# HGRN2 intra-chunk attention in a decoder trunk: the third level's strips run with the fourth level's from kept copies, and the first two levels run in the tick of the first inverse products

## The chip, the cores and the metric

One core of one Trainium2 chip. The metric is the device time of one execution of the whole program, in microseconds (us). All tensors are float32. The large products are done on TensorE in a split form (each operand as a high and a low part, three products per pair), so TensorE's stream of 128x128 by 128x512 matmuls is most of the program.

## What is computed

A decoder layer over 2048 tokens of width 1024 (one layer, batch 1): one input projection feeds four heads of gated DeltaNet and four heads of HGRN2, whose outputs go through one output projection; then an MLP with squared ReLU and a gated embedding. The change lies in the HGRN2 heads. Cut to what matters:

```python
def hgrn2_chunked(q, k, v, log_f):          # here: chunks of 16; the kernel uses chunks of 128
    bc = cumsum(log_f, within the chunk)
    def step(s, (q_n, k_n, v_n, b_n)):
        pair = exp(where(causal, b_n[:, i] - b_n[:, j], -inf))
        att = einsum('bihd,bjhd,bijhd->bhij', q_n, k_n, pair)
        o = att @ v_n + (q_n * exp(b_n)) @ s
        s = s * exp(b_last) + (k_n * exp(b_last - b_n))^T @ v_n
        return s, o
```

The decay between token i and token j has its own value in each of the 128 dimensions, so att is no plain product. The kernel builds it by levels. At level s = 1, 2, 4, ..., 64 a token block of 2s is cut in an early and a late half; queries of the late half meet keys of the early half, each first multiplied by its own decay up to the boundary between the halves. A mask then picks the entries of att that belong to that level.

## The kernel before

**Stages.** An embedding projection, the mixer (the first 1035 us or so), the output projection, the MLP and the gates. The mixer goes through 4 token quarters q of 512 tokens and 4 head pairs h. Each pair (one DeltaNet head and one HGRN2 head, written here as head q_h, so 1_3 is quarter 1, pair 3) has 8 projection works of 24 large matmuls (L1174), in the order k, q, z, v of the DeltaNet head, then f, i, q, g of the HGRN2 head.

**Ticks.** Each work is cut into 3 ticks of 8 large matmuls; a tick thus holds one third of a work, and a pair 24 ticks. Between the large matmuls, `half()` and `tick()` call generators that stand on an agenda: the two head mixers `gdn_mixer` and `hgrn_mixer` of the pair whose projections are running or have just run. The step n of `hgrn_mixer` runs in tick `B_STEPS[n]` and the step n of `gdn_mixer` in tick `A_STEPS[n]`, counted from the tick in which the pair's projections began (the last pair has its own tables `A_LAST`, `B_LAST`, and the first pair has `A_FIRST` for its DeltaNet head). TensorE's order is thus written by hand. SyncE's (SP's) queue, which issues the DMAs, is written by hand in the mixer too. The orders of VectorE (DVE) and ScalarE (ACT) are set when the program is built, by the tile scheduler; they are fixed lists when the program runs.

**The steps of `hgrn_mixer` around the change.** 
- Tick 24 copies the late queries of level 0 to `both[:, 0]` (tile `hb`), and does the first products on DVE. Tick 26 copies the late queries of level 1 to `both[:, 1]`.
- Tick 28 is a bunch of strips for levels 0 and 1. A strip is a small matmul (`strip`, L631) that uses 32 of TensorE's 128 columns: four of them with different column positions fill four row groups of a PSUM tile. Level 0's diagonal goes to `of_h` (4 strips), and its other part and level 1 go to `at_all` (16 strips; 4 and 16 calls give 8 and 32 matmul records in the profile, since a matmul on float32 data shows as two records). Then DVE takes `of_h` (L901) and `at_all` (L903, both with a mask), multiplies the keys by the decay (L926), copies level 1 into att under a mask (L931), multiplies the queries (L930), and forms the decays of the next level (L937). ACT copies the keys for the next level to a packed tile `keys` (L929; this tile has two buffers).
- Tick 30 (level 2, s = 4) and tick 32 (level 3, s = 8) each run 8 strips from `keys` and the queries, and then the same DVE and ACT operations for the next level. Levels 4 to 6 follow in ticks 34, 36 and 38.
- In the DeltaNet head, tick 30 holds the 8 strips `psp5` (a product for the inverse of a triangular matrix) and tick 32 holds the 12 strips `pst5` and `psx5` of the next step of that inverse. In the first pair `psp5` is in tick 32 and the other two in tick 34. In the last pair (`A_LAST`, `B_LAST`) levels 0 and 1 are in tick 26, level 2 in tick 27, level 3 and `psp5` in tick 28.

So in most pairs there are three bunches of strips in these ticks: levels 0 and 1 alone; `psp5` and level 2; `pst5`, `psx5` and level 3. `at_all` is one PSUM bank of 512 columns. A level uses half of it (`lev % 2`), so level 2 and level 3 use different halves.

**Others that run in the same ticks.** DVE and ACT also do the convolution of the DeltaNet projections (L565 on ACT, L569 on DVE, then L570 on DVE and L578 or L575/L576 on ACT), the splits into high and low parts (L176 on ACT, L177 on DVE: of the weights `w` in the first quarter, when they come from HBM, and of the squared head outputs `hl`), the norms (L286, L667, L669, L620) and, from quarter 1 on, `down_sums` (L1128 to L1135), which loads blocks of w_down by DMA and adds and subtracts them on DVE for the MLP. Its calls stand on the agenda at fixed ticks of their own.

Of the kernel before, what the change touches and what calls it, by code (L numbers as in the profile page):

```python
# [13 lines left out]
U32 = mybir.dt.uint32  # L14
AF = mybir.ActivationFunctionType
# [5 lines left out]
P = 128  # L21
# [3 lines left out]
QT = 512  # L25
# [31 lines left out]
           + tuple(o for c in range(38, 54, 4) for o in (c, c + 1.5, c + 2.5))  # L57
           + (53, 55, 57, 59, 60, 61, 65, 66))
I_STEPS = (22,)
B_STEPS = (24, 26, 28, 30, 32, 34, 36, 38, 40, 42, 44, 45, 46, 48, 50, 52, 53, 54, 58, 59)  # L60


A_AHEAD = (-12, -6)
# [33 lines left out]
def trunk(ctx, tc, x, xT, pT, vecs, w_in, w_ab, gdn_a_log, gdn_dt_bias, w_out, w_up, w_down,  # L97
# [363 lines left out]
    with mixers as mctx:  # L461
# [164 lines left out]
        def rows_of(g):  # L626
            return slice(g * SB, (g + 1) * SB)

        def strip(g, out, lhsT, rhs):

            PE.matmul(out, lhsT, rhs, start=True, stop=True, tile_position=(0, g * SB))  # L631
# [223 lines left out]
        def hgrn_mixer(q, h, live):  # L855
# [14 lines left out]
            def by_half(t, s):  # L870
                return t.rearrange("p (a n s) -> p a n s", a=2, s=s)
# [10 lines left out]
            for lev, s in enumerate(LEVELS):  # L882
# [4 lines left out]
                if lev == 1:  # L887
# [6 lines left out]
                    for c in range(NC):  # L894
                        for j in range(NB):
# [31 lines left out]
                if 2 * s < P:  # L927
                    keys = m2.tile([P, QT // 2], F32, tag="keys", name=f"keys_{n}_{lev}")
                    S.activation(keys.rearrange("p (n a s) -> p a n s", a=2, s=2 * s), side(k, QT, 2 * s, False), AF.Copy)  # L929
                V.tensor_tensor(side(qq, QT, s, True), side(qq, QT, s, True), early, ALU.mult)  # L930
                V.copy_predicated(side_of_chunks(columns_of, s, True),  # L931
                                  mask[lev].rearrange("p (a n s) -> p a n s", a=2, s=s).bitcast(U32)[:, :, None]
                                  .broadcast_to([P, 2, 2, P // (2 * s), s]),
                                  ps.rearrange("p a b (n s) -> p a b n s", s=s))
                gv = g.rearrange("p (n two) -> p n two", two=2)
                g2 = mt(f"gg_{n}_{lev}", f"gg{lev}", 1, (P, nb // 2))
                V.tensor_tensor(g2, gv[:, :, 0], gv[:, :, 1], ALU.mult)  # L937
# [1045 lines left out]
```

## Time and profile before

| what | value |
|---|---|
| median of 3 runs | 2637.18 us |
| lowest and highest run | 2633.91 and 2642.8 us |
| the profiled execution, its own time | 2643.16 us |
| its span in the trace | 2641.4 us |
| PE busy | 2601.6 us (98%) |
| DVE, ACT busy | 1964.7 us (74%), 1464.2 us (55%) |
| POOL busy | 137.2 us (5%) |
| granted TensorE clock | 1.000 |

Busy shares are means over the whole program. The change acts only in the mixer, so what matters there is the order on PE, and who is waited for at the strips. In rows of the timeline, the columns are the start in us, the time from the first start to the last end of the group in us, the engine, the line and operation, out<-in, the shape and the number of instructions; a bracket at the end is the idle time just before on that engine, and what ended it. Matmuls are pipelined, so the time of a stretch of n large matmuls contains one tail of about 0.4 us, and starts are compared with starts.

### The profile page before, as it was taken

What the parts mean: (1) busy time and instruction counts of PE and PEld (TensorE: products, weight loads), DVE (VectorE), ACT (ScalarE), POOL (GpSimd) and SP (SyncE); (2) the same over time, 40 slices, a digit from 0 to 9 for tenths busy, and PEclk for the clock granted to TensorE, in tenths of its full rate; (3) what the DMA queues carried; (4) which work ended last, traced back from release to release, by engine and by line L of the source; (5) the groups of instructions that cost most, each with busy time, mean ns of one, the idle gap of its engine ahead of it and who ended that gap; (6) DMA issues with size and microseconds to landing.
All of it is one profiled execution on the core that took longest, in us unless ns stands there. A gap on an engine that the chain in (4) does not pass through costs nothing.

```text
span 2641.4 us, 43911 instructions
## 1 busy us (share of the span) xinstructions
PE 2601.6 (98%) x15593; PEld 2143.3 (81%) x15593; DVE 1964.7 (74%) x4032; ACT 1464.2 (55%) x2991; POOL 137.2 (5%) x147
## 2 busy tenths in 40 slices
PE   8999999999999999999999999999999999999999
PEld 5788788878878888787888888888888888888887
DVE  7788777776777777578988778767877765477776
ACT  7675655465555555566566465555455465565322
POOL 0000000000000000110000000001000001101000
PEclk9999999999999999999999999999999999999999
DMA  8777777767767675774675576665644375677664
GB/s 278 276 266 259 253 264 247 239 215 253 242 201 250 228 233 165 222 211 142 216 230 185 183 231 221 214 211 187 220 151 168 138 245 188 200 253 251 204 218 134
DMA packets 267788, 573.87 MB, mean 217 GB/s; under 512 B 55578, under 2 KB 60152, under 8 KB 250416
## 3 DMA queue, kind: packets, MB, share of 16 engines
q1 hardware_dynamic: 265264, 566.86, 64.5%
q0 software_dynamic: 2304, 4.20, 0.9%
q8 instruction: 123, 2.02, 0.3%
q14 instruction: 97, 0.79, 0.1%
HBM read 410.57 MB, written 160.37 MB: 216 GB/s over the span
## 4 chain that ended last, share of the span: by engine, by line
PE 76%; DMA 10%; DVE 7%; ACT 3%; issue 3%; SPq 1%; POOL 0%; DVEq 0%; ACTq 0%; POOLq 0%
PE d L1208 23%; PE u L1208 23%; PE mm L1174 17%; PE mmg L1208 7%; DMA cache_in<-w 2%; DMA sys_g<-ud_g 1%; PE mme L203 1%; DMA ud_g<-u_g 1%; DMA raw_out<-in_w_out_dram 1%; DMA mixT<-mixd 1%; DMA xs<-in_x_dram 1%; DMA yod<-yo 1%; DVE w L177 1%; DVE pr_g L744 0%; DMA wd<-in_w_down_dram 0%
## 5 line engine op out<-in xcount | busy, mean ns | idle before, releaser
L1174 PE MATMUL mm<-xt,w 128*128 128x512 f32 x3072 | 785.6, 401 | 2.6 <-DVE acc_vg L569 1.3
L1174 PEld LDWEIGHTS mm<-xt,w 128*128 128x128 f32 x3072 | 552.6, 188 | 109.1 <-ACT w L176 1.7
L1208 PE MATMUL d<-db,da 128*128 128x512 f32 x2688 | 612.8, 389 | 0.0
L1208 PE MATMUL u<-t,wu 128*128 128x512 f32 x2604 | 591.2, 389 | 0.0
L1208 PEld LDWEIGHTS d<-db,da 128*128 128x128 f32 x2688 | 504.5, 188 | 104.8
L1208 PEld LDWEIGHTS u<-t,wu 128*128 128x128 f32 x2604 | 488.7, 188 | 101.5
L230 DVE TENSOR_TENSOR db<-db 128x512 fp32r<-128x512 f32 x224 | 159.5, 712 | 62.0 <-ACT db L229 60.9
L1606 DVE TENSOR_TENSOR u<-u,u 128x512 f32<-128x512 f32 x224 | 150.5, 683 | 52.7 <-PE u L1208 51.2
L229 ACT ACTIVATE db<-db 128x512 fp32r<-128x512 f32 x224 | 140.9, 629 | 69.1 <-DMA db<-hid 66.7
L1208 PE MATMUL mmg<-h2T,wg 128*128 128x512 f32 (+1 forms) x792 | 174.7, 383 | 0.0
L1208 PEld LDWEIGHTS mmg<-h2T,wg 128*128 128x128 f32 x792 | 145.5, 188 | 29.1
L1649 ACT ACTIVATE u<-u 128x512 f32<-128x512 f32 x128 | 80.8, 631 | 155.0 <-DVE u L1606 154.5
L177 DVE TENSOR_TENSOR da<-da 128x512 fp32r<-128x512 f32 x128 | 94.5, 738 | 91.8 <-ACT da L176 89.9
L176 ACT ACTIVATE da<-da 128x512 fp32r<-128x512 f32 x128 | 80.6, 630 | 129.0 <-DMA da<-sumd 110.9
L1208 PE MATMUL mmo<-mixT,w_out 128*128 128x512 f32 x600 | 138.9, 391 | 3.6 <-DVE w_out L177 1.6
L1208 PEld LDWEIGHTS mmo<-mixT,w_out 128*128 128x128 f32 x600 | 112.1, 188 | 29.4 <-DVE w_out L177 2.9
L176 ACT ACTIVATE wu<-a 128x512 fp32r<-128x512 f32 x124 | 75.1, 623 | 53.3 <-DMA a<-in_w_up_dram 51.5
L177 DVE TENSOR_TENSOR wu<-a,wu 128x512 fp32r<-128x512 f32 x124 | 86.0, 695 | 8.0 <-ACT wu L176 7.5
L177 DVE TENSOR_TENSOR da<-dr,da 128x512 fp32r<-128x512 f32 x96 | 68.3, 711 | 22.4 <-ACT da L176 21.0
L1650 ACT ACTIVATE u<-u 128x512 f32<-128x512 f32 x128 | 80.4, 628 | 3.0
L246 POOL TENSOR_TENSOR acc_y<-acc_y,sq_y 128x512 f32<-128x512 f32 x28 | 37.6, 1341 | 759.9 <-ACT sq_y L245 759.9
L176 ACT ACTIVATE da<-dr 128x512 fp32r<-128x512 f32 x96 | 60.5, 630 | 29.4 <-DMA dr<-in_w_down_dram 21.1
(401 smaller groups left out, 3677.2 us busy)
## 6 DMA issues: line engine op xcount, KB each, us to landing
w<-cache_in SPq DMA_DIRECT2D x96, 1024.0 KB
db<-hid SPq DMA_DIRECT2D x224, 256.0 KB
cache_in<-w SPq DMA_DIRECT2D x32, 1024.0 KB
hid<-u SPq DMA_DIRECT2D x128, 256.0 KB
da<-sumd SPq DMA_DIRECT2D x128, 256.0 KB
a<-in_w_up_dram SPq DMA_DIRECT2D x124, 256.0 KB
hid<-ht SPq DMA_DIRECT2D x96, 256.0 KB
dr<-in_w_down_dram SPq DMA_DIRECT2D x96, 256.0 KB
```

The source lines that it names most:

```text
L176: S.activation(t[:, 0], raw, AF.Copy)
L177: eng.tensor_tensor(t[:, 1], raw, t[:, 0], ALU.subtract)
L203: PE.matmul(ps, a, b, start=i == 0, stop=i == n - 1)
L229: S.activation(t[:, 0], plain(t), AF.Copy)
L230: V.tensor_tensor(t[:, 1], plain(t), t[:, 0], ALU.subtract)
L246: eng.tensor_tensor(acc, acc, sq, ALU.add)
L1174: PE.matmul(ps, *terms[i], start=i == 0, stop=i == nt - 1)
L1208: PE.matmul(ps, a, b, start=start, stop=stop)
L1606: V.tensor_tensor(c[new], c[old], ps, ALU.add)
L1649: S.activation(c[k], c[k], AF.Relu)
L1650: S.activation(c[k], c[k], AF.Square)
```

## The change

Three things in `hgrn_mixer` and its table.

1. `B_STEPS` begins with 24, 27, 30, 31, 32 where it began with 24, 26, 28, 30, 32. The copy of level 1's late queries goes from tick 26 to 27, the bunch of levels 0 and 1 from tick 28 to 30, and level 2's step from tick 30 to 31. The later ticks are as before. `B_LAST` is not changed.
2. Level 2's step issues no strips. Instead ACT copies the late queries of level 2 to `both[:, 0]`, which level 0 has used (new line L907; 256 columns, 16 such copies in the program), and the name `first_keys` holds on to level 2's keys. The DVE products and the ACT copy of the keys for level 3 follow as before.
3. Level 3's step first runs level 2's 8 strips, from the kept keys and the copied queries, into the half of `at_all` that level 2 always had, then its own 8 strips. DVE then copies both levels into att under their masks, one after the other.

```diff
-B_STEPS = (24, 26, 28, 30, 32, 34, 36, 38, 40, 42, 44, 45, 46, 48, 50, 52, 53, 54, 58, 59)
+B_STEPS = (24, 27, 30, 31, 32, 34, 36, 38, 40, 42, 44, 45, 46, 48, 50, 52, 53, 54, 58, 59)
...
+                elif lev == 2:
+                    S.activation(by_half(both[:, 0], s), side(qq, QT, s, True), AF.Copy)
+                    ps, first_keys = None, keys
                 else:
 
+                    if lev == 3:
+                        for c in range(2):
+                            for j in range(NB):
+                                at_j = both.offset + c * P // 2 + j * SB // 2
+                                strip(j, second[rows_of(j), :, c, near[j]], first_keys[:, c * P + j * SB : c * P + (j + 1) * SB],
+                                      bass.AP(both.tensor, at_j, [list(both.ap[0]), [P, 2], [1, SB // 2]]))
...
-                V.copy_predicated(side_of_chunks(columns_of, s, True),
-                                  mask[lev].rearrange("p (a n s) -> p a n s", a=2, s=s).bitcast(U32)[:, :, None]
-                                  .broadcast_to([P, 2, 2, P // (2 * s), s]),
-                                  ps.rearrange("p a b (n s) -> p a b n s", s=s))
+                if lev == 2:
+                    second = at_all[:, : QT // 2].rearrange("p (a b n) -> p a b n", a=2, b=2)
+                else:
+                    picked = [(lev, s, ps)]
+                    if lev == 3:
+                        picked.insert(0, (2, LEVELS[2], second))
+                    for l, s_l, ps_l in picked:
+                        V.copy_predicated(side_of_chunks(columns_of, s_l, True),
...
```

The number of strips, of masked copies and of products is as before. Behind the change the lines are shifted: the keys' product L926 is L935, the keys' copy L929 is L938, the queries' product L930 is L939, the masked copy L931 is L947, the large matmul L1174 is L1190, and L1131 to L1135 of `down_sums` are L1147 to L1151.

**PE, head 0_1.** Before, in the ticks 28 to 32 of the head (`mm_0` and `mm_12` are projection works of the next pair, whose large matmuls are the stream; `at_all_81` and `of_h_86` are the two PSUM tiles; the numbers behind a name count its tiles):

```order
L1174 MATMUL mm_0_0_2_1998<-xt0_5_547,w_0_0_2_1830 128x512
L631 MATMUL of_h_86<-att_h0_1_1935,one_102 32x4x16 x4
L631 MATMUL at_all_81<-hb_h0_1_1936,qk_h0_1_1659 32x2x16 x16
L1174 MATMUL mm_0_0_2_1998<-xt0_5_547,w_0_0_2_1830 128x512 x2
...
L1174 MATMUL mm_12_0_2_2093<-xt0_2_498,w_12_0_2_1907 128x512 x2
L631 MATMUL psp5_g0_1_2104<-xn_g0_1_1976,um5_584 32x32 x8
L631 MATMUL at_all_81<-qk_h0_1_1659,keys_h0_1_1_2046 32x2x16 x8
...
L631 MATMUL psx5_g0_1_2180<-part5_586,xt_g0_1_1975 32x32 x2
L631 MATMUL at_all_81<-qk_h0_1_1659,keys_h0_1_2_2126 32x2x16 x8
```

And now, over the same ticks:

```order
L1190 MATMUL mm_0_0_2_1998<-xt0_5_547,w_0_0_2_1831 128x512 x3
...
L1190 MATMUL mm_12_0_2_2065<-xt0_2_498,w_12_0_2_1908 128x512 x2
L631 MATMUL psp5_g0_1_2076<-xn_g0_1_1977,um5_584 32x32 x8
L631 MATMUL of_h_86<-att_h0_1_1936,one_102 32x4x16 x4
L631 MATMUL at_all_81<-hb_h0_1_1937,qk_h0_1_1660 32x2x16 x16
...
L631 MATMUL psx5_g0_1_2173<-part5_586,xt_g0_1_1976 32x32 x2
L631 MATMUL at_all_81<-hb_h0_1_1937,keys_h0_1_1_2112 32x2x16 x8
L631 MATMUL at_all_81<-qk_h0_1_1660,keys_h0_1_2_2138 32x2x16 x8
```

Three places where strips break into the large matmuls have become two; the first of these now holds `psp5` with levels 0 and 1, the second holds levels 2 and 3.

**ACT, head 0_1.** Before, from the first keys' copy of the head (for level 2) to the third (for level 4) and what follows; `w_16` is a weight that is split in these ticks, `osq` and `hl` are of a DeltaNet head of the pair before:

```order
L929 ACTIVATE keys_h0_1_1_2046<-qk_h0_1_1659 128x2x32x4
L611 ACTIVATE osq_g0_0_2069<-of_g_85 128x512
L929 ACTIVATE keys_h0_1_2_2126<-qk_h0_1_1659 128x2x16x8
...
L176 ACTIVATE hl_g0_0_2073<-osq_g0_0_2069 128x512
L785 ACTIVATE part5_586<-psp5_g0_1_2104 32x2x32 x4
L929 ACTIVATE keys_h0_1_3_2209<-qk_h0_1_1659 128x2x8x16
L176 ACTIVATE w_16_0_2_2086<-raw_16_0_2_1994 128x1024
L286 ACTIVATE osq_g0_0_2069<-nrm_g0_0_2144 1x512
L667 ACTIVATE jk_g0_2_0_2159,ssk_g0_2_2150<-t_kg0_2_2153 128x128
```

And now:

```order
L176 ACTIVATE hl_g0_0_2045<-osq_g0_0_2041 128x512
L785 ACTIVATE part5_586<-psp5_g0_1_2076 32x2x32 x4
L907 ACTIVATE hb_h0_1_1937<-qk_h0_1_1660 128x256
L176 ACTIVATE w_16_0_2_2058<-raw_16_0_2_1994 128x1024
L578 ACTIVATE y_qg0_2_2057<-acc_qg0_2_2050 128x512
L938 ACTIVATE keys_h0_1_1_2112<-qk_h0_1_1660 128x2x32x4
L286 ACTIVATE osq_g0_0_2041<-nrm_g0_0_2130 1x512
L667 ACTIVATE jk_g0_2_0_2152,ssk_g0_2_2143<-t_kg0_2_2146 128x128
...
L938 ACTIVATE keys_h0_1_2_2138<-qk_h0_1_1660 128x2x16x8
```

The keys' copies for levels 2 and 3 have moved from ahead of the split of `w_16` to behind it, with the convolution's L578, the norm's L286 and four L667 (three of them are left out above) between the new query copy and the second keys' copy.

**DVE, head 1_3.** Before, around the keys' product for level 3 (which is the second L926 of the head); `gcol`, `tail` are gate values of the next quarter, and the block sums of `down_sums` (L1131) come behind the last row shown here:

```order
L926 TENSOR_TENSOR qk_h1_3_6296<-qk_h1_3_6296,gg_h1_3_1_6697 128x2x32x4
L569 SCALAR_TENSOR_TENSOR acc_kg2_0_6730<-mm_4_2_0_6646,cols_96,acc_kg2_0_6730 128x511
L930 TENSOR_TENSOR qk_h1_3_6296<-qk_h1_3_6296,gg_h1_3_1_6697 128x2x32x4
L570 TENSOR_TENSOR acc_kg2_0_6730<-acc_kg2_0_6730,bound_582 128x3
L931 COPY_PREDICATED att_h1_3_6577<-cst_93,at_all_81 128x2x32x4
L549 COPY gcol_2_6800<-ps_gb_2_6795 128x144
L926 TENSOR_TENSOR qk_h1_3_6296<-qk_h1_3_6296,gg_h1_3_2_6777 128x2x16x8
```

And now:

```order
L569 SCALAR_TENSOR_TENSOR acc_kg2_0_6708<-mm_4_2_0_6652,cols_96,acc_kg2_0_6708 128x511
L903 TENSOR_TENSOR att_h1_3_6584<-at_all_81,cst_93 128x2x128
L570 TENSOR_TENSOR acc_kg2_0_6708<-acc_kg2_0_6708,bound_582 128x3
L935 TENSOR_TENSOR qk_h1_3_6303<-qk_h1_3_6303,gg_h1_3_0_6586 128x2x64x2
L947 COPY_PREDICATED att_h1_3_6584<-cst_93,at_all_81 128x2x64x2
L939 TENSOR_TENSOR qk_h1_3_6303<-qk_h1_3_6303,gg_h1_3_1_6769 128x2x32x4
L549 COPY gcol_2_6799<-ps_gb_2_6794 128x144
L1147 TENSOR_TENSOR wd6_1_6703<-wd6_1_6703,wd6_0_6702 128x512
L935 TENSOR_TENSOR qk_h1_3_6303<-qk_h1_3_6303,gg_h1_3_1_6769 128x2x32x4
```

The work of level 1 and the keys' product for level 3 have moved behind the third L569, and the first block sum of `down_sums` (L1147, which is L1131 before) now stands ahead of the keys' product for level 3.

More of the change, by code (lines that the diff above doesn't have):

```diff
@@ L930, in hgrn_mixer @@
                 V.tensor_tensor(side(qq, QT, s, True), side(qq, QT, s, True), early, ALU.mult)
-                V.copy_predicated(side_of_chunks(columns_of, s, True),
-                                  mask[lev].rearrange("p (a n s) -> p a n s", a=2, s=s).bitcast(U32)[:, :, None]
-                                  .broadcast_to([P, 2, 2, P // (2 * s), s]),
-                                  ps.rearrange("p a b (n s) -> p a b n s", s=s))
+                if lev == 2:
[6 more added lines that the diff above has]
+                        V.copy_predicated(side_of_chunks(columns_of, s_l, True),
+                                          mask[l].rearrange("p (a n s) -> p a n s", a=2, s=s_l).bitcast(U32)[:, :, None]
+                                          .broadcast_to([P, 2, 2, P // (2 * s_l), s_l]),
+                                          ps_l.rearrange("p a b (n s) -> p a b n s", s=s_l))
                 gv = g.rearrange("p (n two) -> p n two", two=2)
```

## The prediction

> **What bounds the kernel now.** I read the page first: the span, the engines' busy shares, the granted clock and the chain that ended last, then the group of the mixer's large matmuls.
>
> ```profile
> span 2641.4 us, 43911 instructions
> PE 2601.6 (98%) x15593; PEld 2143.3 (81%) x15593; DVE 1964.7 (74%) x4032; ACT 1464.2 (55%) x2991; POOL 137.2 (5%) x147
> PEclk9999999999999999999999999999999999999999
> PE 76%; DMA 10%; DVE 7%; ACT 3%; issue 3%; SPq 1%; POOL 0%; DVEq 0%; ACTq 0%; POOLq 0%
> L1174 PE MATMUL mm<-xt,w 128*128 128x512 f32 x3072 | 785.6, 401 | 2.6 <-DVE acc_vg L569 1.3
> ```
>
> PE is busy for 98% of the span at full granted clock, and its 3072 large matmuls of the mixer wait only 2.6 us in all. So a change here pays by what it takes out of PE's own stream, and costs by every wait it puts in: there are few waits now, and those of the strips are mostly hidden. The next view is PE's timeline through the three bunches of one ordinary head (1_1).
>
> ```profile
> 412.91 1.16 PE L1174 MATMUL mm<-xt,w 128*128 128x512 f32 x4
> 414.00 0.32 PE L631 MATMUL of_h<-att_h,one 128*32 128x64 f32 x8
> 414.14 0.48 PE L631 MATMUL at_all<-hb_h,qk_h 128*32 128x32 f32 x32
> 414.54 1.19 PE L1174 MATMUL mm<-xt,w 128*128 128x512 f32 x4
> ...
> 416.16 3.02 PE L1174 MATMUL mm<-xt,w 128*128 128x512 f32 x12
> 419.11 0.33 PE L631 MATMUL psp_g<-xn_g,um 128*32 128x32 f32 x16
> 419.25 0.31 PE L631 MATMUL at_all<-qk_h,keys_h 128*32 128x32 f32 x16
> 419.50 2.09 PE L1174 MATMUL mm<-xt,w 128*128 128x512 f32 x8
> ...
> 422.24 2.10 PE L1174 MATMUL mm<-xt,w 128*128 128x512 f32 x8
> 424.27 0.28 PE L631 MATMUL pst_g<-xt_g,part 128*32 128x32 f32 x9
> ...
> 424.78 1.43 PE L1174 MATMUL mm<-xt,w 128*128 128x512 f32 x5
> ```
>
> And the first head, whose level 2 stands alone, with a long stretch ahead of it:
>
> ```profile
> 97.76 7.89 PE L1174 MATMUL mm<-xt,w 128*128 128x512 f32 x34
> ...
> 106.12 3.92 PE L1174 MATMUL mm<-xt,w 128*128 128x512 f32 x16
> 109.97 0.33 PE L631 MATMUL at_all<-qk_h,keys_h 128*32 128x32 f32 x16
> 110.23 2.11 PE L1174 MATMUL mm<-xt,w 128*128 128x512 f32 x8
> ```
>
> One step of the stream is (7.89 - 0.40) / 33 = 0.227 us, with 0.40 for the last one (the group's mean of 401 ns). What a bunch costs is the time from the start of the stretch ahead to the start of the stretch behind, less 0.227 per large matmul. Levels 0 and 1 alone: 414.54 - 412.91 - 4 x 0.227 = 0.72. `psp5` with level 2: 419.50 - 416.16 - 12 x 0.227 = 0.62. `pst5`, `psx5` and level 3: 424.78 - 422.24 - 8 x 0.227 = 0.72. Level 2 alone: 110.23 - 106.12 - 16 x 0.227 = 0.48. Sixteen strip records take 0.14 (419.11 to 419.25), so 0.34 of that 0.48 is paid for breaking into the stream at all, however many strips follow.
>
> **The change part by part.** *PE.* No strip is added or removed; one break of three goes. After it, tick 30 should cost 0.62 - 0.14 + (0.72 - 0.34) = 0.86 and tick 32 0.72 + 0.14 = 0.86: together 1.72 where 2.06 stood, so **0.34 us less per head**. In the last head the lone level 2 bunch goes with a wait of its own:
>
> ```profile
> 1024.80 0.33 PE L631 MATMUL at_all<-qk_h,keys_h 128*32 128x32 f32 x16 [0.56 <-ACT keys_h L929]
> ```
>
> That is 0.34 + 0.56 = 0.90. Gross gain: 15 x 0.34 + 0.90 = **6.0 us**, if nothing new is late.
>
> *What gets tighter.* Before, the strips of levels 0/1, 2 and 3 stood two ticks apart each, and each level's products and key copy had two ticks. Now everything from the first masked product (L901) to the keys of level 3 has to pass between tick 30 and tick 32, some 5 us, through DVE, ACT, DVE and ACT in turn, in fixed queues that also carry the convolution and the splits. Step lengths on DVE, from start to start:
>
> ```profile
> 415.72 0.72 DVE L931 COPY_PREDICATED att_h<-cst,at_all 128x256 f32<-128x256 uint32 x1
> 416.25 0.31 DVE L830 SCALAR_TENSOR_TENSOR S_g<-S_g,cd_g,psc_g 128x128 f32<-128x128 f32 x1
> ...
> 418.28 0.74 DVE L569 SCALAR_TENSOR_TENSOR acc_qg<-mm,cols,acc_qg 128x509 f32<-128x509 f32 x1
> 418.94 0.41 DVE L926 TENSOR_TENSOR qk_h<-qk_h,gg_h 128x256 f32<-128x256 f32 x1
> 419.27 0.68 DVE L177 TENSOR_TENSOR hl_g<-osq_g,hl_g 128x512 fp32r<-128x512 f32 x1
> ```
>
> A convolution step L569 takes 0.66, a 256-column product 0.33, level 1's masked copy 0.53, a split of `hl` 0.60 (0.68 less the same 0.08 of overlap). In head 1_1 DVE's new order from the first L569 is L569, L177, L569, L901, L569, L903, L570, then the keys' product, the masked copy and the two products of the next level: 3 x 0.66 + 0.60 + 5 x 0.33 + 0.07 + 0.53 = 4.8. The stream reaches this L569 about 0.7 earlier than before (levels 0 and 1 no longer break it), near 417.6, so the last product ends near 422.4, and the second key copy near 422.8. The strips of level 2 come behind `pst5` near 423.9. So in 1_1 about 1 us is left and the saving stands. I replayed each head in this way. Eight (1_0, 1_1, 1_2, 2_1, 2_2, 3_0, 3_1, 3_2) come out without a wait, though 2_1 and 3_1 with 0.1 us left, since two block sums of `down_sums` stand in their chain: 8 x -0.34 = **-2.7**. The last head gives **-0.9**.
>
> *Head 0_1: ACT.* The weight split waits for its DMA, and the key copies that ran ahead of it now stand behind it.
>
> ```profile
> 171.91 0.42 ACT L929 ACTIVATE keys_h<-qk_h 128x256 f32<-128x256 f32 x1
> 174.05 1.06 ACT L176 ACTIVATE w<-raw 128x1024 fp32r<-128x1024 f32 x1 [1.72 <-DMA cache_in<-w]
> 175.13 0.59 ACT L286 ACTIVATE osq_g<-nrm_g 1x512 f32<-1x512 f32 x1
> 175.63 0.25 ACT L667 ACTIVATE jk_g<-t_kg 128x128 bf16<-128x128 f32 x1
> ...
> 176.63 1.09 ACT L669 ACTIVATE kt_g<-t_kg,tail_g 128x128 f32<-128x128 f32 x4
> 177.62 0.62 ACT L578 ACTIVATE y_qg<-acc_qg 128x512 f32<-128x512 f32 x1
> ```
>
> New order behind the split's end near 175.1: L578 0.53 (it overlaps its successor), key copy 0.33, L286 0.50 (175.13 to 175.63), four L667 1.00 (175.63 to 176.63), key copy 0.42, so 177.9. The strips of levels 2 and 3 follow, and the next large matmul 0.4 later, near 178.3. Before it started at 176.21:
>
> ```profile
> 176.21 0.96 PE L1174 MATMUL mm<-xt,w 128*128 128x512 f32 x3
> ```
>
> **+2.1.** *Head 0_0: DVE.* The same kind of split, late by its DMA, now stands ahead of the whole chain:
>
> ```profile
> 110.27 1.06 ACT L176 ACTIVATE w<-raw 128x1024 fp32r<-128x1024 f32 x1 [2.32 <-DMA cache_in<-w]
> 111.36 1.23 DVE L177 TENSOR_TENSOR w<-raw,w 128x1024 fp32r<-128x1024 f32 x1 [2.52 <-ACT w L176]
> 115.61 0.73 PE L1174 MATMUL mm<-xt,w 128*128 128x512 f32 x2 [0.55 <-DVE acc_qg L569]
> ```
>
> From 111.36: the split 1.15, three L569 1.98, five products 1.65, a transpose 0.37, L570 0.07, the masked copy 0.53: 117.1; key copy 0.42; strips 0.4: the large matmul at 118.0 where it started at 115.61. **+2.4.**
>
> *Heads 1_3 and 2_3: DMA through DVE.* A block sum that waits for the load of w_down now stands ahead of the product that makes level 3's keys.
>
> ```profile
> 546.25 0.69 DVE L1131 TENSOR_TENSOR wd<-wd,wd 128x512 f32<-128x512 f32 x1 [0.73 <-DMA wd<-in_w_down_dram]
> 545.83 0.96 PE L1174 MATMUL mm<-xt,w 128*128 128x512 f32 x3
> ```
>
> SP issues that load behind another that waits for a scan on DVE; two 0.33 products (L901, L903) leave from ahead of the scan, so the block sum should start near 545.6. It ends at 546.2; product 0.33, key copy 0.42, strips 0.4: 547.4 against 545.83, **+1.55, twice +3.1**. Queued behind the waiting block sum is all of DVE, but PE waits only for this product.
>
> *Heads 0_2, 2_0, 0_3.* In the first two a short wait of about 0.8 (a w split; a DMA'd norm in L620) eats the saving: +0.45 each. In 0_3 PE waits in tick 30 for a transfer, whose time doesn't move, so what was saved ahead of it is lost:
>
> ```profile
> 293.33 0.45 PE L631 MATMUL psp_g<-xn_g,um 128*32 128x32 f32 x16 [1.26 <-DMA xn_g<-xd_g]
> ```
>
> +0.2 there; **+1.1** for the three.
>
> *The new copy.* It has 256 columns, as the key copy at 171.91 (0.42). Sixteen are 6.7 us of ACT, which idles 45% of the span; only where ACT is in the chain (0_1, ahead of the late split) would it count, and there the split's DMA hides it. At worst it costs 0.42 in each of the five heads on which a wait falls, +2.1; at best nothing, which I take. The second masked copy of tick 32 (0.33) stands behind level 4's key product, so it delays no key; if it did, 16 x 0.33 = 5 us at most. The keys' tile has two buffers, and level 4's copy must now wait for level 2's strips; on ACT it stands behind the copy of `pst5`, which waits for the same tick anyway: nothing.
>
> **Sum.** -2.7 - 0.9 + 2.1 + 2.4 + 3.1 + 1.1 = **+5.1 us**. The profiled execution took 2643.16 us (span 2641.4), so it would be 2648.3. The median of the runs is 2637.18, 6.0 lower; +5 on it gives **2642**.
>
> **The rivals.** *More heads wait.* Place: the product and key copy for level 3, in the heads with 0.1 us to spare or a short wait (2_1, 3_1, 2_0, 0_2, 0_3). It decides when the second key copy ends after the `pst5` strips. Two block sums of 0.60, or a split of 1.15, then count in full: 5 x 1.2 = +6, in all +11, 2648 on the median. For it: in 2_1 and 3_1 my sum of ten steps would need to be off by only 0.1 us. Against it: the five chains differ, and all would have to slip.
>
> *The queues hold no one up.* PE collects the 6.0 us: 2631. This needs the split of 0_1 on ACT to be ready before 171.9 and not at 174.05, and the load in 1_3 more than 1.5 us earlier. Single heads may do so (0_1 alone makes +2.7).
>
> *The change doesn't do what it says:* a break costs PE no fixed 0.34, because the cost is in the strips. Then 0.34 x 15 is missing, and +10 follows. The lone bunch of 16 records at 0.48 and the pair of 32 at 0.62 speak against it.
>
> *The clock.* The longest wait of PE among the strips is now 1.26 (0_3), and the granted clock stays in the highest tenth in all 40 slices. The new waits are 1.5 to 3 us long; if such a wait lowered the clock to half for 8 matmuls, 8 x 0.227 = 1.8 us would be added, four times +7: 2649. No row here shows it. [...]
>
> **How the numbers follow.** Forecast (+2 to +8): 0.50. More heads wait: 0.27. Queues hold no one up, or few (-6 to +2): 0.15. No fixed cost: 0.04. Clock: 0.04. A measurement of this kernel tells about 0.3%, or 7.9 us, from no change. The gain of 6 us stays under that, so faster has 0.04 (more gain than worked out); slower takes the two cases near +10, the clock and a small part of the forecast, 0.38; within 0.3% 0.58. Range: from -4 (few waits) to +15 (more waits with copies exposed, or the clock): 2633 to 2652.
>
> **What would show it.** Right: PE has two bunches in ticks 30 and 32, of about 0.86 each in 1_1; 0_1 and 0_0 show over 1.5 us idle ahead of level 2's strips, put down to the key copy on ACT; 1_3 and 2_3 likewise, with the block sum waiting for its DMA ahead of it on DVE; 1_1 shows no wait. Wrong: idle ahead of these strips in 1_1 or 3_0 (more heads), or none in 0_1 (queues free); bunches that cost 1 us or more (no fixed part); slices with a lower clock in the mixer.

## The result, and the profile after

The changed kernel takes 2642.99 us (median of 20 runs, 2636.88 to 2646.9); the kernel before takes 2639.36 (20 runs, 2633.67 to 2642.8). The ratio is **1.0013, 95% interval 1.0007 to 1.0019**: about 3.4 us slower. Beside the kernel before in another job it was 1.0024 (1.0016 to 1.0033), 6.3 us. Both lie within 0.3%, and the runs of either kernel scatter by 9 to 10 us, so the cause has to be read from the ticks themselves. From the page of after:

```profile
span 2640.5 us, 43947 instructions
PE 2600.1 (98%) x15593; PEld 2149.4 (81%) x15593; DVE 1964.1 (74%) x4032; ACT 1470.3 (56%) x3007; POOL 137.2 (5%) x147
```

The page shows no loss: its span is even 0.9 us under that of before, because the profiled execution of before (2643.16) lies 3.8 us above the median of its kernel, and that of after (2642.29) 0.7 under that of its own. First the ordinary head 1_1, on PE:

```profile
416.00 2.97 PE L1190 MATMUL mm<-xt,w 128*128 128x512 f32 x12
418.90 0.33 PE L631 MATMUL psp_g<-xn_g,um 128*32 128x32 f32 x16
419.05 0.30 PE L631 MATMUL of_h<-att_h,one 128*32 128x64 f32 x8
419.16 0.48 PE L631 MATMUL at_all<-hb_h,qk_h 128*32 128x32 f32 x32
419.57 2.11 PE L1190 MATMUL mm<-xt,w 128*128 128x512 f32 x8
...
422.33 2.10 PE L1190 MATMUL mm<-xt,w 128*128 128x512 f32 x8
424.36 0.28 PE L631 MATMUL pst_g<-xt_g,part 128*32 128x32 f32 x9
...
424.74 0.37 PE L631 MATMUL at_all<-qk_h,keys_h 128*32 128x32 f32 x15
425.04 2.35 PE L1190 MATMUL mm<-xt,w 128*128 128x512 f32 x9
```

Two bunches where three stood, and no idle time ahead of the strips. The first costs 419.57 - 416.00 - 12 x 0.227 = 0.85, the second 425.04 - 422.33 - 8 x 0.227 = 0.89. The saving is there. What it is paid with stands in the view of PE's waits over the mixer (100 to 1035 us), after and then before; the columns are the total in us, how often, and the longest:

```profile
PE at_all L631 <- ACT keys_h L938: 6.4, 6, 2.2
PE at_all L631 <- DVE att_h L947: 2.2, 2, 1.7
```

```profile
PE at_all L631 <- DVE att_h L931: 1.0, 3, 0.6
...
PE at_all L631 <- ACT keys_h L929: 0.6, 1, 0.6
```

The strips wait 8.6 us where they waited 1.6. Two of these places on PE's timeline, head 0_0 and head 1_3:

```profile
115.33 0.33 PE L631 MATMUL at_all<-hb_h,keys_h 128*32 128x32 f32 x16 [1.65 <-DVE att_h L947]
116.26 0.33 PE L631 MATMUL at_all<-qk_h,keys_h 128*32 128x32 f32 x16 [0.60 <-ACT keys_h L938]
116.53 4.83 PE L1190 MATMUL mm<-xt,w 128*128 128x512 f32 x13
```

```profile
544.19 0.33 PE L631 MATMUL at_all<-hb_h,keys_h 128*32 128x32 f32 x16
546.73 0.33 PE L631 MATMUL at_all<-qk_h,keys_h 128*32 128x32 f32 x16 [2.21 <-ACT keys_h L938]
547.00 5.29 PE L1190 MATMUL mm<-xt,w 128*128 128x512 f32 x15
```

And DVE in 1_3, where the block sum of `down_sums` stands ahead of the product for level 3's keys:

```profile
545.20 0.69 DVE L1147 TENSOR_TENSOR wd<-wd,wd 128x512 f32<-128x512 f32 x1 [1.32 <-DMA wd<-in_w_down_dram]
545.81 0.42 DVE L935 TENSOR_TENSOR qk_h<-qk_h,gg_h 128x256 f32<-128x256 f32 x1
```

Now the stretch behind each wait. Thirteen large matmuls take 4.83 us in 0_0 and 15 take 5.29 in 1_3, where 0.227 each and a tail of 0.17 would be 3.1 and 3.6. The table of stretches (the last columns are the granted clock, the share of the DMA engines and GB/s) says why:

```profile
113.00:117.00 4.00, 1.74 (x52) 1.12 (x51) 3.01 (x10) 2.86 (x10) 0.88 (x1) 1.00 0.91 354
117.00:121.00 4.00, 4.00 (x13) 3.13 (x12) 3.34 (x11) 3.41 (x8) 0.13 (x1) 0.57 1.03 426
121.00:125.00 4.00, 4.00 (x115) 3.23 (x114) 2.71 (x10) 2.00 (x7) 0.00 (x0) 1.00 0.89 246
542.00:547.00 5.00, 2.52 (x64) 1.72 (x62) 3.62 (x14) 3.61 (x8) 0.00 (x0) 1.00 1.00 414
547.00:551.00 4.00, 4.00 (x20) 3.17 (x12) 3.99 (x10) 3.81 (x11) 0.00 (x0) 0.57 0.94 358
```

**Behind the wait TensorE gets half its clock for some 3.4 us** (0.57 on average over the 4 us; 0.50 from 117.18 to 120.60 in 0_0 and from 547.26 to 550.68 in 1_3). Seven large matmuls take 0.427 us each, 7 x 0.2 = 1.4 us more, and those at the two ends are slow in part; in all, set against the same matmuls before, the clock costs 1.6 us at each place. Head 2_3 shows the same (0.50 from 793.02 to 796.44). The page's row of clock tenths hides it, since one slice of the page is 66 us long.

So that single waits can be set against the forecast, I matched the large matmuls of two traces by their number in the stream, and took by how much their distance grows from just ahead of levels 0 and 1 to 60 large matmuls on (some 20 us, clock included). In us, against the first trace of before; a second trace of before differs from the first by up to 0.8 in quarter 0 and 3_0, by 0.5 in 3_3, and by less than 0.1 in the other heads:

| head | forecast | after, first trace | after, second trace |
|---|---|---|---|
| 0_0 | +2.4 | +3.3 | +3.4 |
| 0_1 | +2.1 | +0.4 | -0.3 |
| 0_2 | +0.45 | -1.0 | -1.1 |
| 0_3 | +0.2 | -0.7 | +0.5 |
| 1_3 and 2_3 | +3.1 | +6.5 | +6.6 |
| 2_0 | +0.45 | -0.3 | +0.7 |
| 1_0 | -0.34 | +0.1 | +0.1 |
| seven others | -2.4 | -1.8 | -1.5 |
| 3_3 | -0.9 | -0.6 | -0.7 |
| sum | +5.1 | +6.0 | +7.8 |

### The profile page after: what moved, and what is told of

It reads as the page before. It is cut to its first block, busy times and chain, and to the rows that moved or that the text cites. A ratio compares the mean times of both kernels' runs of the same rounds, so it can differ in the third digit from the quotient of the medians.

```text
span 2640.5 us, 43947 instructions
## 1 busy us (share of the span) xinstructions
PE 2600.1 (98%) x15593; PEld 2149.4 (81%) x15593; DVE 1964.1 (74%) x4032; ACT 1470.3 (56%) x3007; POOL 137.2 (5%) x147
## 4 chain that ended last, share of the span: by engine, by line
PE 77%; DMA 7%; issue 6%; DVE 6%; ACT 2%; SPq 1%; POOL 0%; DVEq 0%; ACTq 0%; POOLq 0%
PE d L1224 23%; PE u L1224 23%; PE mm L1190 18%; PE mmg L1224 7%; PE mme L203 1%; DMA cache_in<-w 1%; DMA sys_g<-ud_g 1%; DMA xs<-in_x_dram 1%; DMA ud_g<-u_g 1%; DVE pr_g L744 0%; DMA wd<-in_w_down_dram 0%; DMA xd_g<-xs_g 0%; DVE xs_g L746 0%; DVE xt L177 0%; PE psa_g L818 0%
## 5 line engine op out<-in xcount | busy, mean ns | idle before, releaser
L1190 PE MATMUL mm<-xt,w 128*128 128x512 f32 x3072 | 786.2, 402 | 1.4 <-DVE acc_vg L569 1.3
L1190 PEld LDWEIGHTS mm<-xt,w 128*128 128x128 f32 x3072 | 557.4, 189 | 107.9 <-ACT w L176 1.7
```

What stands on the lines that cost most here:

```text
L1190: PE.matmul(ps, *terms[i], start=i == 0, stop=i == nt - 1)
```

## The experiments

Theory A: a break into the stream for strips costs about 0.3 us by itself, and the loss sits in the few heads where level 3's keys come late, with a lower clock behind the longest waits. Rival B: later transfers, which land at their own times, set the pace, so that neither savings nor waits in these ticks come through. Rival C: a break costs nothing by itself. Every ratio is against the kernel before in the same job (medians there 2640.79, 2642.05 and 2640.86 us).

**Four heads as before.** The heads 0_0, 0_1, 1_3 and 2_3 take the old ticks and the old level 2.

```diff
+APART = ((0, 0), (0, 1), (1, 3), (2, 3))
...
-                elif lev == 2:
+                elif lev == 2 and joined:
```

> The changed kernel, but the heads 0_0, 0_1, 1_3 and 2_3 keep the old ticks and the old separate bunches. Theory A (a break into the stream costs about 0.3 us whatever follows it; the loss sits in the few heads where level 3's keys come late, with a lower clock behind the longest waits): the eleven other ordinary heads keep their 0.3 us each and the last head its 0.6, so about 4 us under the kernel before (2635 where before is 2639), 7 us under the changed kernel, no 7 matmuls at 0.43 us in the mixer, and the granted clock of before. Rival B (waits in the mixer are made good later by transfers that land at their own times): the time of the changed kernel moves by less than 2 us. Rival C (a break costs nothing by itself): the time of the kernel before within 1 us.

Measured: 2640.22 us, 0.9999 (0.9989 to 1.0009). The slow matmuls in the mixer are gone, and the mean granted clock of the 11 runs is 0.9988, against 0.9978 in the 20 runs of the changed kernel and 0.9990 in the 27 of before. So the loss goes with these heads, as A has it, but 4 us under before did not come. Head 0_2 shows one reason. ACT and PE in this run:

```profile
231.03 1.06 ACT L178 ACTIVATE w<-raw 128x1024 fp32r<-128x1024 f32 x1 [1.96 <-DMA cache_in<-w]
...
236.35 0.44 ACT L941 ACTIVATE keys_h<-qk_h 128x256 f32<-128x256 f32 x1
```

```profile
236.19 0.33 PE L633 MATMUL at_all<-hb_h,keys_h 128*32 128x32 f32 x16 [1.18 <-DVE att_h L950]
236.84 0.33 PE L633 MATMUL at_all<-qk_h,keys_h 128*32 128x32 f32 x16 [0.32 <-ACT keys_h L941]
```

and ACT in the changed kernel:

```profile
231.18 1.06 ACT L176 ACTIVATE w<-raw 128x1024 fp32r<-128x1024 f32 x1
...
236.65 0.41 ACT L938 ACTIVATE keys_h<-qk_h 128x256 f32<-128x256 f32 x1
```

The stream reaches this head 2 us earlier than in the changed kernel. But the weight split starts at 231.03, after 1.96 us of waiting for its DMA, and in the changed kernel ACT comes to it at 231.18 and does not wait. So the keys come only 0.3 us earlier, and PE waits 1.5 us ahead of levels 2 and 3, 1.18 of it for a masked copy on DVE. Here rival B holds: what is gained ahead of such a split is given back at it. A second place is head 2_2, where level 4's strips wait 0.89 us for a masked copy; the last run below shows that wait.

**The joined bunch two ticks later.**

```diff
-B_STEPS = (24, 27, 30, 31, 32, 34, 36, 38, 40, 42,
+B_STEPS = (24, 27, 30, 31, 34, 36, 38, 39.5, 40.5, 42,
```

> The changed kernel with the bunch of levels 2 and 3 at tick 34 and not 32 (levels 4, 5 and 6 at 36, 38 and 39.5, the transpose of the keys at 40.5), so that the chain from the first masked product to level 3's keys has four ticks where it had two; the last head as in the changed kernel. Theory A: no head waits for level 3's keys, all 15 ordinary heads save 0.3 us and the last 0.6: about 5 us under the kernel before (2634), 8 to 9 under the changed one, clock as before. Rival B: within 2 us of the changed kernel. A third way: levels 5 and 6 and the transpose, now 1 to 1.5 ticks apart, wait in turn; then PE idles ahead of the strips at tick 38 or 39.5 and the time stays at or above that of before.

Measured: 2642.19 us, 1.0007 (0.9997 to 1.0016), clock as before (0.9991 on average). No ordinary head waits for level 3's keys and none shows slow matmuls. Nine heads stand at -0.6 us 45 large matmuls on, which is ahead of the joined bunch, and at -0.3 to -0.4 behind it. But level 5's strips have left the bunch of `pst6` and need a break of their own in tick 38, and level 6's full-width records moved to tick 39.5: by tick 41 seven of the nine stand between -0.1 and +0.2. The saved break was moved, not saved.

**The block sums three ticks later.**

```diff
-        starts = [per_q * q + 5 + n * i for q, m, n in
+        starts = [per_q * q + 5 + n * i + (3 if i == 0 else 0) for q, m, n in
```

> The changed kernel with the first block of the sums over w_down in each quarter three ticks later, so that its wait for the load no longer stands ahead of the product for level 3's keys in heads 1_3 and 2_3. Theory A: in these two heads the wait of 2.2 us falls to about 0.6 (what head 0_3 shows), and no slow matmuls follow; each head gains 3.4 to 4 us, of which about 1 was given back later: 5 to 6 us under the changed kernel in all (2637). Rival B: less than 2 us. If only the wait mattered and the clock followed something else, slow matmuls stay behind 1_3 and 2_3 and the gain is 3 us.

Measured: 2648.54 us, 1.0029 (1.0019 to 1.0039). At the place itself A is right: 1_3 and 2_3 stand at +0.2 and +0.5 where the changed kernel has +3.1 and +3.4, with no slow matmuls. But the edit moved the loads too, in SP's hand-written queue: in quarter 1 they now stand at another place among the weight loads, and the stream loses 3.3 us between 0_3 and 1_0. As a test of the total this run is spoilt by its own edit.

**One break more in the kernel before.**

```diff
+                        if lev == 2 and c == 1:
+                            yield
                         start = qq.offset + c * P + s
```

The second half of level 2's strips gets a tick of its own in the tables, 31 (27.5 in the last head).

> The kernel before with level 2's eight strips cut in two: four in tick 30 with psp5 as before, four by themselves in tick 31, in all 16 heads; no strip is added. Theory A: one more break in each head at 0.3 us fixed: 16 x 0.3 = 5 us over the kernel before (2644); level 2's products come one tick later, and level 3's strips in tick 32 may wait in a head or two, up to 3 us more. Rival C (the cost is in the strips, not in the break): no more than 1 us over the kernel before.

Measured: 2647.38 us, 1.0024 (1.0013 to 1.0035), 6 us slower. PE in head 1_1:

```profile
419.35 0.33 PE L631 MATMUL psp_g<-xn_g,um 128*32 128x32 f32 x16
419.50 0.25 PE L631 MATMUL at_all<-qk_h,keys_h 128*32 128x32 f32 x8
...
422.17 0.27 PE L631 MATMUL at_all<-qk_h,keys_h 128*32 128x32 f32 x8
```

The same 16 records in two places put the stream back by 0.28 to 0.31 us in nine heads of the later quarters. Rival C is out: **a break costs 0.3 us**, and 15 x 0.3 = 4.5 is most of the 6.

**Two block sums on GpSimd.** `first` is GpSimd in the first block of quarters 2 and 3, and VectorE in the others. The loads stay where they are.

```diff
-            V.tensor_tensor(a22, a22, a21, ALU.add)
-            V.tensor_tensor(a21, a11, a21, ALU.subtract)
+            first.tensor_tensor(a22, a22, a21, ALU.add)
+            first.tensor_tensor(a21, a11, a21, ALU.subtract)
```

> The changed kernel; in two blocks of the sums over w_down (the first of quarters 2 and 3) the first two adds run on GpSimd instead of VectorE, with every transfer where it was. Theory A: the wait for the load no longer stands on VectorE ahead of the product for level 3's keys in heads 1_3 and 2_3; their wait of 2.2 us falls to about 0.5 (the rest of the chain, as in 0_3), no slow matmuls follow there, each head gains about 3 us and keeps about 2 of them behind the next transfers: 4 us under the changed kernel, level with the kernel before or 1 to 2 us under it. Rival B (later transfers set the pace anyway): within 2 us of the changed kernel.

Measured: 2646.58 us, 1.0024 (1.0011 to 1.0036). PE in 1_3:

```profile
546.57 0.33 PE L631 MATMUL at_all<-qk_h,keys_h 128*32 128x32 f32 x16 [0.89 <-ACT keys_h L938]
546.84 3.94 PE L1190 MATMUL mm<-xt,w 128*128 128x512 f32 x16
...
552.26 0.33 PE L631 MATMUL at_all<-qk_h,keys_h 128*32 128x32 f32 x16 [1.13 <-DVE att_h L947]
```

and DVE there:

```profile
549.33 0.69 DVE L1150 TENSOR_TENSOR wd<-wd,wd 128x512 f32<-128x512 f32 x1 [3.09 <-POOL wd L1148]
```

The wait falls from 2.21 to 0.89, and 16 matmuls take 3.94 us (full clock). But the next block sum on DVE now waits 3.09 us for GpSimd, the two masked copies of levels 2 and 3 stand behind it, and level 4's strips wait 1.13 for the second. The wait has moved one tick on. The total did not fall, so nothing was won.

**Quarter 0 as before, and the two sums.** The run above, with all four heads of quarter 0 as before.

```diff
+APART = ((0, 0), (0, 1), (0, 2), (0, 3))
```

> As the run with the two blocks on GpSimd, and the four heads of quarter 0 with the old ticks and separate bunches. Theory A2 (in quarter 0 the chain hangs on weight splits that wait for their transfer, so the stream cannot get ahead there and a saved break is worth nothing; from quarter 1 on each saved break is worth 0.3 us): at the end of quarter 0 the stream stands where it stands in the kernel before; then ten heads save 0.3 us, two about nothing and the last 0.6: about 3 us under the kernel before (0.9989), the best version of these. Rival: 0 to 1 us, if the later quarters give it back too.

Measured: 2644.36 us, 1.0013 (1.0003 to 1.0022). The first half holds: at head 1_0 the stream stands at -2.2 us against the first trace of before, and the second trace of before at -2.8. The second half doesn't: the sums on GpSimd cost their waits in 1_3 and 2_3, and it ends above before.

**Levels 0 and 1 back in tick 28**, the other part of the change kept.

```diff
-B_STEPS = (24, 27, 30, 31, 32,
+B_STEPS = (24, 26, 28, 30, 32,
```

> One part undone: levels 0 and 1 alone in tick 28 as before, level 2's step without strips in tick 30, levels 2 and 3 joined in tick 32; the last head as in the changed kernel. Theory A: no break is saved in the 15 ordinary heads (16 strip records go from the bunch in tick 30 to the one in tick 32, 0 us), the keys have four ticks and no head waits; only the last head gains 0.6: the time of the kernel before, to 1 us under it. If the extra query copies and the joined masked copies cost something by themselves, it is slower than before by what they cost.

Measured: 2645.07 us, 1.0019 (1.0009 to 1.0030), slower than expected. In the heads it is as expected (+0.05 us in eight of them, no wait for keys). In the trace the loss, 2 to 8 us by the interval, lies outside these ticks, at waits for transfers that differ from trace to trace. What in this version makes them longer is open.

**A stair of waits in the kernel before.**

```diff
+HOLD = {(1, 1): 12, (1, 2): 14, (2, 0): 16, (2, 1): 18, (2, 2): 20, (3, 0): 22, (3, 1): 24, (3, 2): 26}
...
+                    for _ in range(HOLD.get((q, h), 0)):
+                        V.tensor_copy(keys, keys)
```

> The kernel before with idle copies of level 3's keys onto themselves on VectorE (256 columns, about 0.3 us each; 12, 14, 16, 18, 20, 22, 24 and 26 of them in the heads 1_1, 1_2, 2_0, 2_1, 2_2, 3_0, 3_1, 3_2), so that the strips of tick 32 wait longer from head to head, from under 1 us to about 5 us. Theory A (a wait of TensorE over about 2 us is followed by some 3.4 us at half clock): heads with a wait up to about 1.5 us show the step of 0.227 us right behind it, heads with more than about 2 us show 6 to 9 matmuls at 0.43 us, and the number of slow matmuls does not grow with the wait. Rival (the slow matmuls behind 1_3 and 2_3 come from something else at those places, a transfer or a load of the chip's power): no slow matmuls here, since none of these heads had any.

Measured: 2702.79 us (one run). The waits came out longer than meant, 3.1 to 8.4 us, so the short steps are missing. Behind each of the eight stand 5 to 11 slow matmuls. Head 1_1, the shortest, as rows of PE and as the stretch behind the wait:

```profile
426.58 0.37 PE L632 MATMUL at_all<-qk_h,keys_h 128*32 128x32 f32 x16 [3.10 <-DVE keys_h L933]
426.88 5.46 PE L1178 MATMUL mm<-xt,w 128*128 128x512 f32 x16
```

```profile
426.50:430.50 4.00, 3.92 (x25) 3.13 (x26) 1.46 (x6) 0.83 (x2) 0.00 (x0) 0.57 1.03 246
```

At these places no other trace has slow matmuls. So the wait brings the lower clock, not the place.

**The kernel before again.**

> The kernel before once more, for a second trace of it: which waits outside the strips (for transfers that land at times of their own) stand in both traces at the same place and with the same length, and which differ. If they differ by some 3 us in sum, a single pair of traces cannot be used to balance the account outside the ticks 28 to 32, and only the medians can.

Measured: 2646.4 us (one run). In the ticks 28 to 32 of quarters 1 to 3 the two traces of before agree within 0.01 us up to 3_2. Outside they do not: PE waits ahead of level 6 in 2_0 and 3_0 for a convolution on DVE that stands behind a norm from a DMA.

```profile
625.26 0.68 PE L913 MATMUL at_all<-qk_h,keys_h 128*128 128x128 f32 x4 [2.58 <-DVE acc_vg L570]
```

```profile
876.92 0.68 PE L913 MATMUL at_all<-qk_h,keys_h 128*128 128x128 f32 x4 [2.75 <-DVE acc_vg L570]
```

The first trace had 1.53 us at the first place and no wait at the second. These two alone make 4 us between two executions of one kernel, which is why single traces cannot close the account outside the ticks.

**The changed kernel again.**

> The changed kernel once more, for a second trace and beside the others of this job. Theory A: the waits of over 2 us ahead of the strips of tick 32 in 0_0, 1_3 and 2_3 are there again, with 6 to 9 matmuls at 0.43 us behind each; eight heads show -0.3 us; the median lies 3 us over the kernel before of this job. Rival (those three waits were chance landings of transfers): other heads, or none.

Measured: 2648.33 us, 1.0024 (1.0016 to 1.0033). The same three heads wait and are followed by 7, 5 and 7 slow matmuls; what each head costs is in the last column of the table above. The rival of chance landings is out for them. But only five heads show -0.3 where eight were expected, and the median lies 7.5 us over that of before, not 3.

**The query copies alone.**

```diff
+                if lev == 2:
+                    S.activation(by_half(both[:, 0], s), side(qq, QT, s, True), AF.Copy)
```

> The kernel before with nothing but the 16 extra copies of level 2's queries on ScalarE, which nobody reads, so that the queries' product waits for the copy as in the changed kernel. My prediction put them at nothing: within 1.5 us of before. Rival D, after the run with levels 0 and 1 back in tick 28, which saved no break and was 5 us slower in the median: the copy and the product's wait for it cost by themselves, then 2 to 5 us over before. If it is within 1.5 us, what that run lost lies in the joined bunch (level 4's strips wait for level 2's masked copy, which now comes two ticks later) or in the landing of transfers.

Measured: 2639.69 us, 0.9999 (0.9990 to 1.0008). Rival D, that the added query copies cost 2 to 5 us, is out but for its lowest end, since the interval ends 2.1 us over before: the copies cost nothing that shows. What the run with levels 0 and 1 back in tick 28 lost is then in the joined bunch or in the landing of transfers; these two were not separated.

**Six heads as before.**

```diff
+APART = ((0, 0), (0, 1), (0, 2), (0, 3), (1, 3), (2, 3))
```

> The changed kernel with six heads as before: the four of quarter 0, whose pace the weight splits set, and 1_3 and 2_3, whose keys wait behind the load of w_down. Nine ordinary heads and the last keep the change. Theory A2: no new wait over 1 us, nine times 0.3 and once 0.6 saved: 3 us under before. If it is not under before, the 0.3 us are given back behind transfers in the later quarters too, as rival B has it, and no version of this change is worth anything.

Measured: 2642.22 us, 1.0007 (0.9994 to 1.0019). Seven of the nine heads stand at -0.3 us behind tick 32, and the other two, 1_0 and 2_0, wait 0.18 and 0.76 us for keys; 3 us under before are outside the interval. In 2_2 a wait of 0.96 us stands that the two traces of after have with 0.12 and 0.27, shown here on PE and then on DVE:

```profile
734.55 0.30 PE L633 MATMUL at_all<-qk_h,keys_h 128*32 128x32 f32 x13 [0.96 <-DVE att_h L950]
```

```profile
731.54 0.75 DVE L622 SCALAR_TENSOR_TENSOR og_h<-og_h,cols,rsb_h 128x512 f32<-128x512 f32 x1 [2.48 <-DMA rsb_h<-rd_h]
...
733.99 0.42 DVE L950 COPY_PREDICATED att_h<-cst,at_all 128x256 f32<-128x256 uint32 x1
```

DVE stands 2.48 us for a norm that a DMA brings back, and everything of this step queues behind it: the masked copies of levels 2 and 3 and the product for level 4's keys. The second masked copy ends at 734.41, and the key copy on ACT (734.16, 0.42 long, not shown) at about the same time; level 4's strips start behind both. Both masked copies now stand between ticks 32 and 34, where before only level 3's did. Whether the strips wait for the half of `at_all` that level 2 used or for the tile as a whole was not tried. So the joined step leaves less time for the next one, and a transfer that lands late there is paid for by PE. The median is above that of the kernel before, though within the interval.

## Why the prediction came out

The time, its sign and the range were right, and most of the mechanism; two of its terms were wrong in opposite directions. That 2642.99 lies within 1 us of the forecast 2642 is in part luck. The forecast stood on a median of 3 runs, 2.2 us under that of 20, and the two wrong terms nearly cancel: without the clock quarter 0 lost about 1.7 us where 5.15 were forecast, and the clock, which the sum left out, took 4.6 to 4.8.

*The saved break* was 0.34 in the forecast and is 0.3. Seven of the eight heads that were to save it without a wait gave 1.5 to 1.8 us in all, against 2.4 forecast. Of these 2_2 lost its share ahead of level 4, where the strips wait for a masked copy; 1_0 lost it to a load that ACT waited for.

*1_3 and 2_3* were right in mechanism and nearly in time: the block sum was put at 545.6 and started at 545.20, the large matmul at 547.4 and started at 547.00. Up to that matmul each lost 1.8 us in the first trace and 2.0 in the second, against 1.55; the clock came on top.

*0_0* was right in its chain and too large: +2.4 forecast, +1.7 and +1.8 before the clock. The long wait there is put down to a masked copy on DVE and not to the key copy on ACT, as the forecast had it.

*0_1 failed.* The large matmul was put at 178.3 and started at 178.02:

```profile
177.76 0.33 PE L631 MATMUL at_all<-qk_h,keys_h 128*32 128x32 f32 x16 [0.50 <-ACT keys_h L938]
178.02 3.93 PE L1190 MATMUL mm<-xt,w 128*128 128x512 f32 x16
```

But the stream came to this head 1.4 us later than before, with what 0_0 had lost. The wait of over 1.5 us that was to be the sign of this term is 0.50 us here, and the second trace has none. The step that failed is the sum: I added the heads as if each started from its time in the old trace. Both end at a weight split that a DMA times (in 0_1 it starts at 173.90, and before at 174.05), so the second pays only what the first has not. The same holds for 0_2 and 0_3. The four heads of quarter 0 were forecast at +5.15. At head 1_0, three traces with the changed quarter 0 (both of after and the one with two sums on GpSimd) stand at +0.5, +1.5 and +3.2, and seven with the old one (two of before, the stair, which begins only in 1_1, one with an added break, the copies alone, and two with quarter 0 undone) at 0, -2.8, -1.3, -0.1, -2.8, -2.2 and -2.0: 3.3 us apart on average.

*The clock* was a rival with a chance of 0.04, and it came true in three heads: 1.6 us each (once 1.4 in the second trace), 4.8 and 4.6 us in all. I had set it aside because the longest wait among the strips before, 1.26 us in 0_3, left the clock alone. Half the clock for 8 matmuls, 1.8 us a wait, was an assumption that no row of before shows; in the first trace of after each of the three waits is followed by 7 large matmuls at 0.427 us, in the second by 7, 5 and 7. The runs agree with the size: the mean granted clock is 0.9978 (20 runs) and 0.9975 (11 runs) for the changed kernel and 0.9987 to 0.9990 for that of before; 0.0012 of 2640 us is 3.2 us, about the first measured difference and half of the second. Waits of 2.2 us, with strips on both sides, were enough here (2.21 us in 1_3, then 0.50 of the clock for 3.4 us); the last section shows what decided.

*Not foreseen:* that level 4's strips can wait for the two masked copies of the joined step (1_3 with two sums on GpSimd, 2_2 with six heads as before). I had looked only at the keys that stand behind these copies on DVE, not at who waits for the copies themselves.

*The rival of more heads waiting* (2_1, 3_1, 2_0, 0_2, 0_3) did not come: 2_1 and 3_1 held, their keys ready 0.15 and 0.25 us ahead of the strips in the first trace. 0_3 waits 0.63 us in both traces, 2_0 0.76 and 0_2 0.31 in the second alone, short waits as the forecast gave 0_2 and 2_0. That queues hold no one up, and that a break costs nothing, are both excluded. The rest of the account stays open: outside the ticks the traces differ by some 3 us either way, and why the version with levels 0 and 1 back in tick 28 is 2 to 8 us slower was not settled.

## What to carry to other kernels

Joining bunches of strips saved 0.3 us per break here, but only where the chain that feeds the joined bunch had time: count every step of that chain through the fixed queues, and look for a step that stands behind a transfer. Waits that ended at transfers did not add up from stage to stage (quarter 0 lost about 1.7 us before the clock, where 5.15 were forecast), and savings ahead of them were lost too (in 0_2 with four heads as before, the stream came 2 us earlier and the keys 0.3). A TensorE wait of 2 us can cost more than its length: behind the 2.21 us in 1_3 the matmuls ran at half clock, 0.427 us each, which cost 1.6 us more. Here the lower clock followed every step of 3.41 us with 1.9 us or more of idle time, and one with 1.69.

## What the runs showed of the hardware

The lower clock behind a wait. In the mixer of all fourteen traces the granted clock is whole (1.00) or half (0.50). It changes only at the borders of steps of 3.413 us, whose grid holds through a trace: in the first trace of after half clock begins at 117.18, 547.26 and 793.02 us, 126 and 72 steps apart. The grid does not lie alike in all traces: the border at 626.22 below, in the second trace of before, is 0.45 us off the grid of that one. Half clock lasts one such step (117.18 to 120.60, for one), and up to three at the longest waits of the stair (there 0.50 over 960 to 969 us, and 0.94 over 969 to 973). What decided in these traces is not the length of a wait but the idle time of PE inside one step. The second trace of before has two waits of nearly one length; here they are by the steps of its grid (the columns are the stretch, its length, the busy time of PE, of its weight loads, of DVE, ACT and POOL, then the granted clock, the share of the DMA engines and GB/s):

```profile
622.81:626.22 3.41, 0.96 (x6) 0.93 (x7) 3.38 (x8) 1.33 (x4) 0.00 (x0) 1.00 1.03 392
626.22:629.64 3.42, 3.42 (x9) 2.65 (x8) 3.32 (x9) 1.60 (x3) 0.00 (x0) 0.50 0.23 78
...
871.98:875.40 3.42, 2.19 (x11) 1.68 (x9) 2.12 (x4) 0.00 (x0) 0.00 (x0) 1.00 1.00 392
875.40:878.81 3.41, 1.89 (x10) 1.68 (x11) 3.34 (x8) 2.23 (x6) 0.00 (x0) 1.00 0.82 297
878.81:882.23 3.42, 3.42 (x22) 2.95 (x21) 3.21 (x13) 2.48 (x5) 0.00 (x0) 1.00 0.53 137
```

Nearly all of the wait of 2.58 us lies in one step, which has 3.41 - 0.96 = 2.45 us idle, and the next step has half clock. The longer wait of 2.75 us is cut by a border into 1.23 and 1.52 us, and the clock stays whole. Counted over the mixers of the fourteen traces, 18 steps at whole clock have 1.9 us or more of idle time, and half clock follows each of them (2.16, 2.30 and 2.42 us in 0_0, 1_3 and 2_3 of the first trace of after). Below that it follows once, behind 1.69 us; it does not follow the seven other steps from 1.5 to 1.88 us, nor any with less. So two waits of 1.65 and 0.60 us close together in 0_0 lower the clock (2.16 us in one step), and one of 2.76 us in the run with one break more does not (1.88 at most in one). Where a wait lies on the grid counts, then: 2.58 us inside one step lowered the clock, and 2.75 us cut by a border did not.

A break cost 0.3 us for strips, and less for full-width matmuls. Two full-width 128x128 records between two stretches of large matmuls cost 441.91 - 438.95 - 12 x 0.227 = 0.24 us, their own work included (`psb_g` in the kernel before):

```profile
438.95 2.98 PE L1174 MATMUL mm<-xt,w 128*128 128x512 f32 x12
441.77 0.39 PE L823 MATMUL psb_g<-r_g,xt_full 128*128 128x128 f32 x2
441.91 1.17 PE L1174 MATMUL mm<-xt,w 128*128 128x512 f32 x4
```

while the added break costs its 0.3 with no strip added.
